# Spilled tiles reloaded four steps ahead, 24 modulation columns moved to the first stage, eight more early tiles in the first placing

## The chip, the cores and the metric

The kernel runs as one program on one core of a Trainium2 chip. The metric is the device time of one execution in microseconds (us); before the change it is 2992.85 us, the median of three runs (2987.78 to 2998.39). All sizes are fixed: 512 tokens and a width of 1024.

## The reference, cut to what matters

Two transformer blocks follow each other. The first mixes tokens by differential attention and a gated linear recurrence, and then runs an expert layer (PEER): every token takes 8 x 16 of 16384 experts, and each expert is one row of `peer_u` and one row of `peer_v`. The second block is modulated by a vector `c`: nine slices of `silu(c) @ w_ada + b_ada` shift, scale and gate its three parts.

```python
def peer_ffn(h, w_query, subkeys, u_table, v_table):      # one block of 128 tokens
        ...                                               # experts and gates by two top-16 searches
        u = u_table[experts]
        hid = jax.nn.gelu(jnp.einsum('nkd,nd->nk', u, xb).astype(jnp.float32), approximate=False) * gates
        return jnp.einsum('nk,nkd->nd', hid.astype(xb.dtype), v_table[experts])
...
    c_act = jax.nn.silu(c)
        mod = c_act @ w_ada[l] + b_ada[l]
        (sh1, sc1, g1, sh2, sc2, g2, sh3, sc3, g3) = jnp.split(mod, N_MOD, axis=-1)
        h = modulate(rmsnorm_2(x, norm_ffn1[l]), sh1, sc1)
```

## The kernel before

Every dense product is made of three TensorE passes: weights and activations are split into a rounded part and its rest (`whi`/`wlo`, `xh`/`xl`, lines 223 to 235). A weight tile is a 128 x 1024 block of 512 KB. SyncE (SP) issues its load into one of three `raw` buffers, ScalarE (ACT) casts it to `whi` (L226), VectorE (DVE) subtracts to get `wlo` (L227), and TensorE (PE) runs its matmuls.

The **first stage** projects the tokens for four heads (`rec_proj`, four weight tiles a head), then runs attention and the recurrence.

The **expert layer** treats 384 of the 512 tokens densely and the other 128 sparsely. The dense way multiplies all 16384 experts: 128 U tiles (`u_chunk`, 24 matmuls, then a GELU on ACT, L725) and 128 V tiles (`down`, 36 matmuls in pairs, L960). Between them the hidden values `ge` are multiplied with a gate matrix on DVE (L945) and split again (`hh` on ACT, L298; `hl` on DVE, L299). The gate matrix is not there from the start: DVE searches the top 16 (`select`), and `place` writes the gates of four tokens at a time into a dense block `stg` (DVE makes two one-hot blocks, ACT scales, PE multiplies, ACT copies out, L885). Every eight such steps the 2 MB of `stg` are stored to `g_d` in HBM (L887). There are three placings of 32 steps.

So that PE has work meanwhile, 80 of the 128 U tiles are made early and their `ge` spilled to `e_d` (192 KB each, `early_u`): 14 during and after the first search, one at every second placing step (48), and the last 18 after the placings. The **main loop** then goes over 128 tiles. At step i it makes or reloads `ge` of tile i (`hidden`), runs `down(i - 3)`, and takes a share of the sparse part. A reload was issued in the step that uses it, into the pool that also holds the fresh GELU outputs:

```python
                if i in done:
                    ge = tp.tile([P, TD], F, name="ge", tag="w")
                    nc.sync.dma_start(ge, e_d[done[i]])
```

Of each eight tiles the five at places 1, 2, 4, 5 and 7 are spilled. The **sparse part** gathers rows of `u` and `v` for the other 128 tokens: 256 gathers of 512 KB (GpSimd, POOL, L747), each followed by one DVE instruction (L756, L764). `sparse` paces them: 32 by the end of the placings, two with each of the 18 late U tiles, the rest spread over the main loop.

The **modulation columns** are 72 products of a 512 KB tile of `w_ada` with the broadcast `silu(c)` (`ada`: a DMA that ACT issues into a `raw` buffer, one DVE instruction, L672). 24 of them stood in the main loop, 48 in the next stage, the first feed-forward layer. `load_c` loads and activates `c`, once behind the placings and once in front of that layer.

Each engine runs its instructions in one fixed order, which a scheduler makes when the program is built; a wait at the head holds back what is behind it. SP's DMA issues also stand in one such order: all weight tiles, the spills and the reloads.

Of the kernel before, what the change touches and what calls it, by code (L numbers as in the profile page):

```python
# [5 lines left out]
P = 128  # L6
T = 512
NM = 16
TE = T + NM
D = 1024  # L10
# [6 lines left out]
EVU = 2  # L17
TD = T - P
# [4 lines left out]
LAG = 2  # L23
LAG2 = 3
LA = 3
NEG = -1.0e30
LAM_INIT = 0.8 - 0.6 * math.exp(-0.3 * 0)
D_FF = 2816
# [131 lines left out]
def program(tc, A, dbg=None, stop=None):  # L160
    import concourse.bass as bass
    from concourse import mybir
    F = mybir.dt.float32
# [4 lines left out]
    AF = mybir.ActivationFunctionType  # L168
    OP = mybir.AluOpType
    AX = mybir.AxisListType  # L170
    PSUM = bass.MemoryType.PSUM
    nc = tc.nc
# [8 lines left out]
    with root:  # L181
# [35 lines left out]
        lastlo = []  # L217
# [37 lines left out]
        class Norm:  # L255


            def __init__(self, nk, pool=nrm, name="nacc", eng=G):
                self.nk, self.eng = nk, eng
                self.acc = pool.tile([P, T], F, name=name, bufs=1)  # L260
                self.k = 0

            def add(self, src, scale=1.0):
# [40 lines left out]
        def stats(pst, sq, tiles, first, last):  # L304
            for j, (c, n) in enumerate(tiles):
                M.matmul(pst[:n, j:j + 1], sq[:, c:c + n], ones[:, 0:1], start=first and j == 0,
                         stop=last, skip_group_check=True)


        with ExitStack() as es:  # L310
# [212 lines left out]
            def rec_proj(h):  # L523
                o = proj(True)
                n1 = first_norm() if h == 0 else iter(())
                next(n1, None)
                o2 = proj(False)
                next(n1, None)
                f = rp.tile([P, TE], F, name="f")
                scaled(f, o)  # L530
                S.activation(f, f, AF.Sigmoid)
                V.tensor_scalar(f, f, oml[:, h:h + 1], lb[:, h:h + 1], op0=OP.mult, op1=OP.add)

                def silu(dst, o):
                    V.tensor_mul(dst, o, rbs[:, :T])
                    sg = tp.tile([P, T], F, name="sg", tag="w", bufs=4)
                    S.activation(sg, dst, AF.Sigmoid)
                    G.tensor_mul(dst, sg, dst)

                q, rg = qr[:, h], qr[:, 4 + h]  # L540
                silu(q, o2)
                vn = to_nat("vr", rp, 4)
                silu(rg, proj(False))
                rec.append((f, q, vn, rg))

            def hgrn(h):
# [69 lines left out]
                split(mh[:, 4 + h], ml[:, 4 + h], y)  # L616
                dump("rec", y, h)

            for h in range(4):
                rec_proj(h)  # L620
                if h == 0:
                    lvm = cp.tile([P, 8, P], U8, name="lvm")
                    for i in range(2):
                        cst = tp.tile([P, T], F, name="lvs", tag="w", bufs=4)
                        nc.scalar.dma_start(cst, A["levels"][:, i * T:(i + 1) * T])
                        V.tensor_copy(lvm[:, i * 4:i * 4 + 4].rearrange("p a b -> p (a b)"), cst)
# [29 lines left out]

        def res(k):
            return xT[:, k]

        cact = []  # L660

        def load_c(pool):
            cb = pool.tile([P, D], F, name="cb", bufs=1)
            nc.scalar.dma_start(cb, A["c"].to_broadcast([P, D]))
            S.activation(cb, cb, AF.Silu)
            cact[:] = [cb]

        def ada(i0, i1):
            for i in range(i0, i1):
                raw = wraw.tile([P, D], F, name="raw")  # L670
                nc.scalar.dma_start(raw, A["w_ada"][i])
                V.scalar_tensor_tensor(raw, raw, 1.0, cact[0], op0=OP.mult, op1=OP.mult,  # L672
                                       accum_out=mod[:, i:i + 1])

        def bias_mod(i0, i1):
            a0, _ = COL_AT["b_ada"]
# [9 lines left out]
        with ExitStack() as es:  # L686
# [35 lines left out]
            def u_chunk(i):  # L722
                o = gemm8(pa, A["peer_u"][i], xh, xl, "a", TD)
                ge = tp.tile([P, TD], F, name="ge", tag="w")
                S.activation(ge, o[:, :TD], AF.Gelu)  # L725
                return ge

            done = {}
# [37 lines left out]
            def sparse(want, step):  # L766

                want = int(min(want, 2 * P))
                while gat[0] < want or (want == 2 * P and gat[1] < want):
                    if gat[0] - gat[1] > lag[0] or gat[0] == 2 * P:  # L770
                        with tc.issue_after(step.ins):
                            use(gat[1])
                        gat[1] += 1
                    if gat[0] < 2 * P:
                        gather(gat[0])
                        gat[0] += 1
# [124 lines left out]
            for t in range(3):  # L901
                for n, _ in enumerate(place(t)):
                    if t < 2:
                        next(nxt, None)
                    if t == 0 and n % 4 == 0:
                        next(nxt, None)
                    if n % EVU == EVU - 1:
                        early_u()
                    sparse(RW[t][0] + RW[t][1] * (n + 1) / 32, placed[0])
            for _ in nxt:  # L910
# [6 lines left out]
            vd = ExitStack()  # L917
            pv = vd.enter_context(tc.tile_pool(name="p1v", bufs=1, space=PSUM))
            rw2 = es.enter_context(tc.tile_pool(name="p1w2", bufs=GB2))
            load_c(hq)  # L920
            nr, nr2 = Norm(8), Norm(8, hq, "nacc2")
            n0 = NU - len(done)
            for _ in range(n0):
                early_u()
                sparse(gat[0] + 2, lastlo[0])
            sp = gat[0]
            pools = [rwp] * GB + [rw2] * GB2
            lag[0] = LAG2
# [5 lines left out]
            def hidden(i):  # L934

                if i % 4 == 0:
                    nc.scalar.dma_start(gts[:, i // 4 % 2].rearrange("p g i n -> p (g i n)"),
                                        g_d[i // 4].rearrange("j g x -> j (g x)"))
                if i in done:
                    ge = tp.tile([P, TD], F, name="ge", tag="w")  # L940
                    nc.sync.dma_start(ge, e_d[done[i]])
                else:
                    ge = u_chunk(i)
                g3 = ge.rearrange("p (g n) -> p g n", n=TG)
                gated[:] = [V.tensor_mul(g3, g3, gts[:, i // 4 % 2, :, i % 4])]  # L945
                hh_ = hq.tile([P, TD], R, name="hh", bufs=LA + 2)
                hl_ = hq.tile([P, TD], R, name="hl", bufs=LA + 2)
                split_alt(i, hh_, hl_, ge)
                hid[i] = hh_, hl_

            def down(i):

# [2 lines left out]
                for t in range(3):  # L955
                    sl = slice(t * P, (t + 1) * P)
                    for x_, w, st, en in ((hh_, hi, i == 0, False), (hl_, hi, False, False),
                                          (hh_, lo, False, i == P - 1)):
                        for j in range(2):
                            M.matmul(acc[t * 2 + j], x_[:, sl], w[:, j * T:(j + 1) * T], start=st, stop=en,  # L960
                                     skip_group_check=True)

            for i in range(P + LA):
                if i < P:
                    hidden(i)
                if i >= LA:
                    down(i - LA)
                if i < P:
                    ada(24 * i // P, 24 * (i + 1) // P)
                    sparse(sp + (2 * P - sp) * cost[i] / cost[P - 3], gated[0])  # L970
            ys = [rwp.tile([P, D], F, name="rows") for t in range(3)]
            for t in range(3):
                for j in range(2):
                    (V.tensor_copy if j else S.copy)(ys[t][:, j * T:(j + 1) * T], acc[t * 2 + j])
            ys += ya
            vd.close()
            ps = es.enter_context(tc.tile_pool(name="p1e", bufs=2, space=PSUM))
            for m in range(8):
# [498 lines left out]
```

## Time and profile before

| what | before |
|---|---|
| median of three runs | 2992.85 us |
| the profiled execution | 2989.74 us |
| its span, first to last instruction | 2987.9 us |
| mean granted clock of PE in it | 0.972 |
| PE busy | 2813.1 us (94%) |
| DVE busy | 1910.7 us (64%) |
| ACT busy | 1160.2 us (39%) |
| POOL busy | 478.4 us (16%) |
| moved by DMA | 522.25 MB, 175 GB/s on average |

The profile is one execution. A busy share is an average over stages that have different limits. The granted clock is the share of the full rate that the throttle gave PE: 1.00 is 2.4 GHz, half of it 1.2 GHz. An idle time stands in brackets with what ended it: `[4.31 <-DVE wlo L227]` says that the engine had waited 4.31 us for that result.

### The profile page before, as it was taken

The page shows a single profiled execution, that of the slowest core. Times are in us where ns is not written, and L with a number is a line of the kernel's source. Part 1 is how long each engine was busy: PE and PEld are TensorE (multiplying, and loading weights), DVE is VectorE, ACT ScalarE, POOL GpSimd, SP SyncE. Part 2 cuts the span into 40 slices and gives each one's busy share as a digit, 9 for nine tenths or more (in the row PEclk, how much of TensorE's full clock was granted, in tenths as well). Part 3 has the DMA queues.
Part 4 walks back from the last instruction along what each step waited for, and adds up shares of the span by engine and source line. Part 5 has one row for each costly group of instructions (what it writes and reads, how often), then busy time and mean ns, then how long its engine had stood idle before and what let it go on. Part 6 is the DMA issues. An engine that isn't in the chain of part 4 may idle for free. (4 is left out here: it accounts for less than half of the span.)

```text
span 2987.9 us, 37696 instructions
## 1 busy us (share of the span) xinstructions
PE 2813.1 (94%) x14087; PEld 2394.2 (80%) x14087; DVE 1910.7 (64%) x3461; ACT 1160.2 (39%) x2003; POOL 478.4 (16%) x353
## 2 busy tenths in 40 slices
PE   8999999988996899998998997999999999999998
PEld 7878779878996788877877876888878777788876
DVE  5577489999775688766777674554457645533332
ACT  3233333566772233333333334222245626422222
POOL 2000100000133333333334322000110000200000
PEclk9999999999998999999999998999999999999999
DMA  4201223456899899988988862555522102233332
GB/s 146 78 29 36 79 85 113 136 165 197 275 318 345 308 356 340 323 307 290 320 290 312 311 224 85 171 174 173 167 91 74 50 30 64 78 99 93 97 92 73
DMA packets 201303, 522.25 MB, mean 175 GB/s; under 512 B 17184, under 2 KB 88992, under 8 KB 200992
## 3 DMA queue, kind: packets, MB, share of 16 engines
q1 hardware_dynamic: 96480, 290.56, 29.7%
q0 software_dynamic: 36864, 134.23, 12.6%
q10 hardware_dynamic: 67776, 95.04, 9.4%
q8 instruction: 111, 1.82, 0.3%
q14 instruction: 72, 0.59, 0.1%
HBM read 476.78 MB, written 42.99 MB: 174 GB/s over the span
## 5 line engine op out<-in xcount | busy, mean ns | idle before, releaser
L226 ACT CAST whi<-raw 128x1024 fp32r<-128x1024 f32 (+2 forms) x500 | 512.2, 1029 | 904.2 <-PE o L234 579.5
L233 PE MATMUL o<-xh,whi 128*128 128x512 f32 (+1 forms) x2064 | 762.7, 371 | 31.0 <-ACT ge L725 26.7
L235 PE MATMUL o<-xh,wlo 128*128 128x512 f32 (+1 forms) x2064 | 760.5, 369 | 24.7 <-DVE wlo L227 24.5
L227 DVE TENSOR_TENSOR wlo<-raw,whi 128x1024 fp32r<-128x1024 f32 (+2 forms) x500 | 592.4, 1197 | 276.8 <-ACT whi L226 267.6
L234 PE MATMUL o<-xl,whi 128*128 128x512 f32 (+1 forms) x2064 | 759.3, 368 | 1.3 <-DVE xl L1018 0.7
L233 PEld LDWEIGHTS o<-xh,whi 128*128 128x128 f32 x2064 | 395.0, 192 | 79.8 <-ACT ge L725 30.1
L235 PEld LDWEIGHTS o<-xh,wlo 128*128 128x128 f32 x2064 | 394.4, 191 | 71.8 <-DVE wlo L227 30.6
L234 PEld LDWEIGHTS o<-xl,whi 128*128 128x128 f32 x2064 | 394.4, 191 | 47.0 <-DVE xl L1018 2.5
L960 PE MATMUL acc<-wlo,hh 128*128 128x512 f32 x768 | 243.7, 399 | 33.7 <-DVE wlo L227 33.7
L747 POOL DMA_INDIRECT rows<-u_rows,eg x128 | 160.5, 1254 | 690.6 <-DVE rows L756 459.2
L747 POOL DMA_INDIRECT rows<-v_rows,eg x128 | 189.4, 1480 | 346.3 <-DVE ya L764 327.8
L960 PE MATMUL acc<-whi,hl 128*128 128x512 f32 x768 | 241.5, 396 | 2.3 <-DVE hl L299 2.3
L960 PE MATMUL acc<-whi,hh 128*128 128x512 f32 x768 | 242.0, 397 | 1.5 <-ACT hh L298 1.5
L271 POOL TENSOR_TENSOR nacc<-nacc,nsq 128x512 f32<-128x512 f32 x47 | 68.0, 1456 | 1028.8 <-ACT nsq L268 586.2
L298 ACT CAST hh<-ge 128x384 fp32r<-128x384 f32 x128 | 65.8, 514 | 396.3 <-DVE ge L945 388.4
L960 PEld LDWEIGHTS acc<-wlo,hh 128*128 128x128 f32 x768 | 146.5, 192 | 69.7 <-DVE wlo L227 39.4
L672 DVE SCALAR_TENSOR_TENSOR raw<-raw,cb 128x1024 f32<-128x1024 f32 x72 | 89.2, 1238 | 149.6 <-DMA raw<-w_ada 149.6
L756 DVE SCALAR_TENSOR_TENSOR rows<-rows,xn 128x1024 f32<-128x1024 f32 x128 | 155.5, 1221 | 38.2 <-DMA rows<-u_rows,eg 38.0
L960 PEld LDWEIGHTS acc<-whi,hl 128*128 128x128 f32 x768 | 147.3, 192 | 34.3 <-DVE hl L299 2.6
L960 PEld LDWEIGHTS acc<-whi,hh 128*128 128x128 f32 x768 | 147.1, 192 | 29.7 <-ACT hh L298 1.8
L945 DVE TENSOR_TENSOR ge<-ge,gts 128x384 f32<-128x384 f32 x128 | 71.0, 554 | 156.1 <-DMA ge<-e_d 156.1
L764 DVE SCALAR_TENSOR_TENSOR ya<-rows,hg,ya 128x1024 f32<-128x1024 f32 x127 | 162.4, 1279 | 0.0
(455 smaller groups left out, 4076.1 us busy)
## 6 DMA issues: line engine op xcount, KB each, us to landing
raw<-peer_u SPq DMA_DIRECT2D x128, 512.0 KB
raw<-v_rows SPq DMA_DIRECT2D x128, 512.0 KB
raw<-w_ada ACTq DMA_DIRECT2D x72, 512.0 KB
raw<-w_in SPq DMA_DIRECT2D x54, 512.0 KB
g_d<-stg ACTq DMA_DIRECT2D x12, 2048.0 KB
gts<-g_d ACTq DMA_DIRECT2D x32, 768.0 KB
e_d<-ge SPq DMA_DIRECT2D x80, 192.0 KB
ge<-e_d SPq DMA_DIRECT2D x80, 192.0 KB
```

Of the source, the lines that this page charges most:

```text
L226: S.copy(hi[:, :n], raw[:, :n])
L227: lastlo[:] = [V.tensor_sub(lo[:, :n], raw[:, :n], hi[:, :n].bitcast(F))]
L233: M.matmul(out, a, xh, start=first, stop=False, skip_group_check=True)
L234: M.matmul(out, a, xl, start=False, stop=False, skip_group_check=True)
L235: M.matmul(out, b, xh, start=False, stop=last, skip_group_check=True)
L271: self.eng.tensor_add(self.acc, self.acc, sq)
L672: V.scalar_tensor_tensor(raw, raw, 1.0, cact[0], op0=OP.mult, op1=OP.mult, accum_out=mod[:, i:i + 1])
L747: G.indirect_dma_start(out=rw, out_offset=None, in_=A["u_rows" if s < P else "v_rows"], in_offset=bass.IndirectOffsetOnAxis(ap=eg[:, s % P ...
L756: V.scalar_tensor_tensor(rw, rw, 1.0, xn, op0=OP.mult, op1=OP.mult, accum_out=h)
L764: V.scalar_tensor_tensor(ya[0], rw, h, ya[0], op0=OP.mult, op1=OP.add)
L945: gated[:] = [V.tensor_mul(g3, g3, gts[:, i // 4 % 2, :, i % 4])]
L960: M.matmul(acc[t * 2 + j], x_[:, sl], w[:, j * T:(j + 1) * T], start=st, stop=en, skip_group_check=True)
```

## The change

A reload is now issued four steps ahead of its use (`LE = 4`, `reload`) into a pool of its own with four buffers, `ges`. `load_c` is called in the first stage: it puts `silu(c)` into two rows of `qr` that the fourth head fills later. The first 24 modulation columns follow the projections of heads 0, 1 and 2, eight each, and SP issues their loads. The main loop has no `ada` and the placings' end no `load_c` any more. In the first placing a U tile is also made at every fourth step, so that placing has 24 instead of 16, and 10 instead of 18 are left for the time after the placings. There one gather instead of two goes with each of them, so the main loop starts with 42 gathers done instead of 68. The accumulator of the second norm takes a `rows` buffer. The numbers of what is computed do not change.

```diff
+LE = 4
...
+        def load_c(pool, cb=None):
+            if cb is None:
+                cb = pool.tile([P, D], F, name="cb", bufs=1)
+            src = A["c"].to_broadcast([P, D])
+            nc.scalar.dma_start(cb, src if len(cb.shape) == 2 else src.rearrange("p (a t) -> p a t", a=2))
+            S.activation(cb, cb, AF.Silu)
+            cact[:] = [cb]
+
+        def ada(i0, i1, eng=nc.scalar):
+            for i in range(i0, i1):
+                raw = wraw.tile([P, D], F, name="raw")
+                eng.dma_start(raw, A["w_ada"][i])
+                rv = raw if len(cact[0].shape) == 2 else raw.rearrange("p (a t) -> p a t", a=2)
+                V.scalar_tensor_tensor(rv, rv, 1.0, cact[0], op0=OP.mult, op1=OP.mult,
+                                       accum_out=mod[:, i:i + 1])
...
+            load_c(None, qr[:, 3::4])
             for h in range(4):
                 rec_proj(h)
+                if h < 3:
+                    ada(8 * h, 8 * h + 8, nc.sync)
...
-                    if n % EVU == EVU - 1:
+                    if n % EVU == EVU - 1 or t == 0 and n % 4 == 0:
                         early_u()
...
-            load_c(hq)
-            nr, nr2 = Norm(8), Norm(8, hq, "nacc2")
             n0 = NU - len(done)
             for _ in range(n0):
                 early_u()
-                sparse(gat[0] + 2, lastlo[0])
+                sparse(gat[0] + 1, lastlo[0])
...
-                if i in done:
-                    ge = tp.tile([P, TD], F, name="ge", tag="w")
-                    nc.sync.dma_start(ge, e_d[done[i]])
-                else:
-                    ge = u_chunk(i)
+                ge = spilled.pop(i) if i in done else u_chunk(i)
...
+            spilled = {}
+
+            def reload(i):
+                if i in done:
+                    spilled[i] = hq.tile([P, TD], F, name="ges", bufs=4)
+                    nc.sync.dma_start(spilled[i], e_d[done[i]])
...
+            for i in range(LE):
+                reload(i)
             for i in range(P + LA):
+                reload(i + LE)
                 if i < P:
                     hidden(i)
                 if i >= LA:
                     down(i - LA)
                 if i < P:
-                    ada(24 * i // P, 24 * (i + 1) // P)
                     sparse(sp + (2 * P - sp) * cost[i] / cost[P - 3], gated[0])
...
+            nr, nr2 = Norm(8), Norm(8, acc=rw2.tile([P, D], F, name="rows")[:, :T])
```

Three places of the engines' orders show what moves. The first is the start of SP's order, where all loads of the first stage stand; before:

```order
L195 DMA raw<-w_in 128x1024
L199 DMA x0T<-xT 128x528 x8
L223 DMA raw<-w_in 128x1024 x27
L223 DMA raw<-w_out 128x1024 x8
L223 DMA raw<-w_query 128x1024 x16
```

And after:

```order
L196 DMA raw<-w_in 128x1024
L200 DMA x0T<-xT 128x528 x8
L224 DMA raw<-w_in 128x1024 x3
L323 DMA raw<-w_ada 128x1024 x8
L224 DMA raw<-w_in 128x1024 x4
L323 DMA raw<-w_ada 128x1024 x8
L224 DMA raw<-w_in 128x1024 x4
L323 DMA raw<-w_ada 128x1024 x8
L224 DMA raw<-w_in 128x1024 x16
L224 DMA raw<-w_out 128x1024 x8
```

Eight loads of modulation columns now stand in front of the four weight tiles of heads 1, 2 and 3, in the same three `raw` buffers.

The second place is ACT's order at the end of the last placing, from the last copy into `stg` on (`gts` is the gate block that is read back from `g_d`); before:

```order
L885 COPY stg<-pg 128x128x4 x2
L887 DMA g_d<-stg 128x32x128
L725 ACTIVATE ge<-o 128x384
L226 CAST whi<-raw 128x1024 x2
L664 DMA cb<-c 128x1024
L725 ACTIVATE ge<-o 128x384
L937 DMA gts<-g_d 128x1536
L665 ACT_TABLE_LOAD
L665 ACTIVATE cb<-cb 128x1024
L725 ACT_TABLE_LOAD
L725 ACTIVATE ge<-o 128x384 x2
```

And after:

```order
L892 COPY stg<-pg 128x128x4 x2
L894 DMA g_d<-stg 128x32x128
L732 ACTIVATE ge<-o 128x384
L227 CAST whi<-raw 128x1024 x2
L732 ACTIVATE ge<-o 128x384
L942 DMA gts<-g_d 128x1536 x2
L732 ACTIVATE ge<-o 128x384
L227 CAST whi<-raw 128x1024 x2
```

The load of `c`, its activation and two table loads are gone; the read of `gts` comes one GELU later than the load of `c` stood, and nothing but that GELU stands between.

The third place is DVE's order in the middle of the main loop (`hl` is the rest of a gated tile, `ya` the sparse sum; `ge` is a fresh or a reloaded tile before, a fresh one after, where reloaded ones are named `ges`); before:

```order
L945 TENSOR_TENSOR ge<-ge,gts 128x384
L764 SCALAR_TENSOR_TENSOR ya<-rows,hg,ya 128x1024
L299 TENSOR_TENSOR hl<-ge,hh 128x384 x2
L764 SCALAR_TENSOR_TENSOR ya<-rows,hg,ya 128x1024
L945 TENSOR_TENSOR ge<-ge,gts 128x384
L764 SCALAR_TENSOR_TENSOR ya<-rows,hg,ya 128x1024
L227 TENSOR_TENSOR wlo<-raw,whi 128x1024
L299 TENSOR_TENSOR hl<-ge,hh 128x384
L227 TENSOR_TENSOR wlo<-raw,whi 128x1024
L672 SCALAR_TENSOR_TENSOR raw,mod<-raw,cb 128x1024
L227 TENSOR_TENSOR wlo<-raw,whi 128x1024 x2
```

And after:

```order
L300 TENSOR_TENSOR hl<-ges,hh 128x384
L771 SCALAR_TENSOR_TENSOR ya<-rows,hg,ya 128x1024
L300 TENSOR_TENSOR hl<-ges,hh 128x384
L771 SCALAR_TENSOR_TENSOR ya<-rows,hg,ya 128x1024
L228 TENSOR_TENSOR wlo<-raw,whi 128x1024
L771 SCALAR_TENSOR_TENSOR ya<-rows,hg,ya 128x1024
L228 TENSOR_TENSOR wlo<-raw,whi 128x1024
L946 TENSOR_TENSOR ges<-ges,gts 128x384
L228 TENSOR_TENSOR wlo<-raw,whi 128x1024 x2
L946 TENSOR_TENSOR ge<-ge,gts 128x384
L771 SCALAR_TENSOR_TENSOR ya<-rows,hg,ya 128x1024
L300 TENSOR_TENSOR hl<-ge,hh 128x384
```

The L672 row is gone, and the gate multiply of a reloaded tile stands between the `wlo` of weight tiles. Every `hl<-ges` frees one of the four buffers for the reload that is fourth behind it; here the gate multiply next behind the second `hl<-ges` comes two `ya` and two `wlo` later.

## Rows read from the trace of the kernel before

**Rows 1.** Busy time by stretch: start:end, length, then engines, clock, DMA share, GB/s.

```profile
core 0: us, PE busy (x) PEld busy (x) DVE busy (x) ACT busy (x) POOL busy (x), PEclk, DMA share, GB/s
0.00:140.00 140.00, 128.16 (x806) 114.74 (x807) 77.17 (x134) 46.21 (x66) 24.05 (x19) 1.00 0.37 119
551.00:677.00 126.00, 108.01 (x618) 100.56 (x618) 124.89 (x310) 80.98 (x190) 3.46 (x3) 0.93 0.47 148
888.00:1019.00 131.00, 95.99 (x491) 92.15 (x490) 71.10 (x98) 36.27 (x49) 49.48 (x37) 0.90 0.91 324
1019.00:1788.00 769.00, 732.70 (x3407) 632.88 (x3407) 572.29 (x732) 256.37 (x350) 260.97 (x186) 0.98 0.86 310
1100.00:1200.00 100.00, 100.00 (x479) 87.31 (x478) 81.59 (x124) 37.20 (x49) 39.51 (x29) 1.00 0.92 337
```

**Rows 2.** What PE waited for from 888 to 1019 us: total, times, longest.

```profile
PE o L233 <- ACT ge L725: 21.3, 4, 15.0
PE o L235 <- DVE wlo L227: 12.6, 7, 4.8
```

**Rows 3.** ACT's timeline there: start, duration, instruction, idle before and its releaser.

```profile
888.68 0.38 ACTq L887 DMA_DIRECT2D g_d<-stg  x1
...
912.05 0.35 ACTq L664 DMA_DIRECT2D cb<-c  x1
912.45 0.49 ACT L725 ACTIVATE ge<-o 128x384 f32<-128x384 f32 x1 [17.66 <-DMA g_d<-stg]
```

**Rows 4.** SP's timeline there: two rows that follow each other.

```profile
890.26 0.33 SPq L736 DMA_DIRECT2D e_d<-ge  x1
912.03 0.33 SPq L223 DMA_DIRECT2D raw<-v_rows  x1
```

**Rows 5.** The GELUs from 912 to 1019 us: ns min/median/max, first and last start.

```profile
L725 ACT ACTIVATE ge<-o x19: 478/484/492, 912.4 to 1015.7; 128x384 f32<-128x384 f32 x19
```

**Rows 6.** What DVE and PE waited for in the main loop, 1019 to 1788 us.

```profile
DVE ge L945 <- DMA ge<-e_d: 156.1, 42, 7.7
DVE wlo L227 <- ACT whi L226: 34.0, 19, 3.2
...
PE acc L960 <- DVE wlo L227: 33.7, 13, 6.1
```

**Rows 7.** One stall of the main loop in the timeline: SP, PE and DVE.

```profile
1401.50 1.37 SPq L941 DMA_DIRECT2D ge<-e_d  x2
...
1410.33 0.33 PE L233 MATMUL o<-xh,whi 128*128 128x384 f32 x1
...
1413.14 0.56 DVE L945 TENSOR_TENSOR ge<-ge,gts 128x384 f32<-128x384 f32 x1 [7.58 <-DMA ge<-e_d]
...
1414.49 0.62 PE L960 MATMUL acc<-whi,hh 128*128 128x512 f32 x2
...
1419.88 1.22 PE L960 MATMUL acc<-wlo,hh 128*128 128x512 f32 x2 [4.31 <-DVE wlo L227]
...
1420.90 1.05 PE L960 MATMUL acc<-whi,hh 128*128 128x512 f32 x2
```

**Rows 8.** DVE's groups on the page: count, busy us, mean ns, idle before.

```profile
L227 DVE TENSOR_TENSOR wlo<-raw,whi 128x1024 fp32r<-128x1024 f32 (+2 forms) x500 | 592.4, 1197 | 276.8 <-ACT whi L226 267.6
...
L672 DVE SCALAR_TENSOR_TENSOR raw<-raw,cb 128x1024 f32<-128x1024 f32 x72 | 89.2, 1238 | 149.6 <-DMA raw<-w_ada 149.6
L756 DVE SCALAR_TENSOR_TENSOR rows<-rows,xn 128x1024 f32<-128x1024 f32 x128 | 155.5, 1221 | 38.2 <-DMA rows<-u_rows,eg 38.0
```

**Rows 9.** The first stage's timeline: two tiles one head apart, and one load.

```profile
36.73 1.05 ACT L226 CAST whi<-raw 128x1024 fp32r<-128x1024 f32 x1 [4.42 <-PE pj L400]
...
43.84 0.33 ACTq L625 DMA_DIRECT2D lvs<-levels  x1
...
46.39 0.43 DVE L626 CAST lvm<-lvs 128x512 uint8<-128x512 f32 x1 [1.16 <-DMA lvs<-levels]
...
60.19 1.05 ACT L226 CAST whi<-raw 128x1024 fp32r<-128x1024 f32 x1 [4.23 <-PE pj L400]
```

More of the change, by code (lines that the diff above doesn't have):

```diff
@@ L255, in program, with __init__ @@
         class Norm:
-            def __init__(self, nk, pool=nrm, name="nacc", eng=G):
+            def __init__(self, nk, pool=nrm, name="nacc", eng=G, acc=None):
                 self.nk, self.eng = nk, eng
-                self.acc = pool.tile([P, T], F, name=name, bufs=1)
+                self.acc = pool.tile([P, T], F, name=name, bufs=1) if acc is None else acc
                 self.k = 0
@@ L307, in stats @@
                          stop=last, skip_group_check=True)
+        cact = []
+        def load_c(pool, cb=None):
[12 more added lines that the diff above has]
+                                       accum_out=mod[:, i:i + 1])
         with ExitStack() as es:
@@ L658, in res @@
             return xT[:, k]
[L660 to L673, printed above, removed]
         def bias_mod(i0, i1):
```

## The prediction

> **What bounds the kernel now.** I read the busy time by stretch first, then in each stretch that the change touches what ended the waits, and the timeline only where a wait needed a cause. In all of them the reader should look for the engine without idle time, since only its work is on the path.
>
> The first stage is PE's: 128.16 of 140.00 us at clock 1.00, while DVE works 77.17 [rows 1]. The first placing (551 to 677) is DVE's: 124.89 of 126.00, PE 108.01 at 0.93 [rows 1]. Behind the placings (888 to 1019) no engine is full: PE 95.99 of 131.00 at 0.90, but DMA 0.91 and 324 GB/s [rows 1]. That stretch starts with a hole: ACT issues a store of `g_d` at 888.68, has the load of `c` next, which waits for the stores until 912.05, and the GELU behind it starts after 17.66 us of idle time [rows 3]; PE waits up to 15.0 us for that `ge` [rows 2]. SP, too, issues nothing from 890.26 to 912.03 [rows 4]. Then 19 GELUs follow in 103.3 us, 18 intervals of 5.74 us [rows 5].
>
> The main loop (1019 to 1788) has PE busy 732.70 of 769.00 at 0.98 [rows 1]; at full clock and without idle time that work is 732.7 x 0.98 = 718 us, so 51 us are to be had. DVE's 572.29 busy [rows 1], 156.1 waiting for reloads in 42 waits and 34.0 for `whi` [rows 6] make 762 of 769: DVE never has time in hand, because a reload at its head stops it. One stall shows how that reaches PE [rows 7]: reloads issued at 1401.50, DVE released at 1413.14 (11.6 us later), `wlo` late, PE idle 4.31 us and then a pair of matmuls in 1.05 instead of 0.62 us. Where DVE keeps up (1100 to 1200) PE is busy 100.00 of 100.00 at 337 GB/s [rows 1].
>
> **The change part by part.**
>
> *Modulation columns in the first stage.* 24 loads and 24 DVE instructions of 1.238 us [rows 8] = 29.7 us; DVE has 140.00 - 77.17 = 62.8 us free [rows 1], so nothing need show. No wait goes and nothing is taken out here, so it can't be below 0. But eight loads go ahead of each head's four weight tiles through the same three buffers, in a head of 60.19 - 36.73 = 23.46 us; a load of half the size lands 46.39 - 43.84 = 2.55 us after its issue [rows 9]. With the products one after another, 24 x (2.55 + 1.24) = 91 us less the free 63, it is +28. It is nearer to nothing, as DVE's free time is twice its new work; I take one landing seen in each of three heads, 3 x 2.55 = **+8**.
>
> *Eight more U tiles in the first placing.* DVE, the bound, gets eight `wlo`, 8 x 1.197 = 9.6 us [rows 8]. PE gets 8 x 4.16 (one U tile, 1410.33 to 1414.49 [rows 7]) = 33.3 us and has 18.0 idle [rows 1], so with all of these filled it needs 15.3 more. Ends: 9.6 and, with no idle time usable, 33.3. PE and DVE would be about equally full, and a fuller PE may get back part of the 0.93; I take **+14**.
>
> *Behind the placings.* Eight tiles of 5.74 us leave: -45.9. Gathers fall from two with each of 18 tiles to one with each of 10, 26 fewer. The stretch moves 131 us x 324 GB/s = 42.4 MB [rows 1]; 26 gathers of 0.52 MB, eight weight tiles of 0.52 and their spills of 0.2 take 19.4 MB out, at the same rate -60 us. If DMA is no limit any more, 103.3 becomes 10 x 4.16 = 41.6, -62, and the load of `c`, its activation and the table loads leave too: PE's waits for `ge` are 21.3, 15.0 of them the hole [rows 2], so -6.3 at most. The hole stays: the read of `gts` waits for the same stores, one GELU later in ACT's order. Ends: -33 (PE's 8 x 4.16 alone) and -68; I take **-62**, as bytes and PE's floor agree within 8 us.
>
> *Main loop, DVE's work.* Out go 24 products, 24 x 1.238 = 29.7 us; in come the uses of 26 gathers, 26 x 1.221 = 31.7 us [rows 8]. The bytes go the same way, 12.6 MB out and 13.6 in. Nothing either way, and PE covers it: DVE without the reload waits would need 606 of 718 us.
>
> *Main loop, reloads.* Four steps are 24 us (769/128 = 6.0 each), twice the 11.6 us landing. But the pool has four buffers, so a reload can't be issued before the `hl` of the fourth reload before it. I counted DVE's order between that `hl` and the gate multiply which needs the tile: for three of five tiles in each period of eight, two to four instructions, 3 to 5 us; for the other two about 14 us. So two of five land in time, 0.4 x 51 = 20 us, and the other three keep some 8 of their 11.6 us wait, 0.6 x 51 x 0.3 = 9. Ends: 0 and -51; I take **-30**. New on SP: the reload now waits for an `hl` at the head of the queue, with the loads of V and U tiles behind it, and PE waits for these.
>
> Of how long a transfer takes, row and rule differ. The trace shows 11.6 us for a reload of 192 KB under load [rows 7]. The Trainium skill, "DMA: Bandwidth & Descriptors", section "Anatomy of one DMA — SWDGE (gpsimd) path", fits 2.0 us plus bytes / 436e3 for a single DMA issued from GpSimd (these come from SP): an estimate of 2.45 us, by which even the short leads suffice and the loop goes to its floor. By the trace they don't.
>
> The rest (accumulators created later, one in a `rows` buffer) issues nothing in a full stretch.
>
> Sum: 8 + 14 - 62 - 30 = -70. The profiled execution took 2989.74 us, 3.1 below the median of 2992.85, so 2989.74 - 70 + 3.1 = **2923**.
>
> **The rivals.**
>
> *The ring is too short everywhere.* DVE's waits for reloads keep their size since `hl` frees a buffer too late; loop 0. For it: the 3 to 5 us leads. Against: the other two of five. 2923 + 30 = 2953.
>
> *Every reload lands in time.* The 11.6 us of [rows 7] is a peak in a crowded moment, and the usual landing is like the 2.55 us of [rows 9]. Loop -51: 2923 - 21 = 2902. Against: the longest of 42 waits is 7.7, their mean 156.1/42 = 3.7 [rows 6], so ordinary ones are late too. The rule of the Trainium skill weighed above would give this result.
>
> *The first stage is held by its buffers:* +28 instead of +8, 2943.
>
> *The moved U tiles bring nothing:* the placing grows by 33 and the tail loses 33. For it: at 0.93 PE is not idle because of lack of work alone. 2923 + 48 = 2971.
>
> *No effect:* the loop's wait moves from DVE to SP's queue, the tail's bytes only move into the loop. About 2993.
>
> *Slower, by SP's queue.* A reload that waits for `hl` holds the V tile's load behind it. From that `hl` PE has three V tiles of (718 - 48 x 4.16)/128 = 4.05 us and a U tile of 4.16 before the V tile is needed, 16.3 us; landing 11.6, cast 1.05 [rows 9] and `wlo` 1.2 take 13.9. If landing takes over 14 us, PE stalls in each of 16 periods, as in [rows 7]: 4.3 idle and six pairs at 1.05 instead of 0.62, about 7 us; 16 x 7 = +112 in place of -30: 3065. For it: SP did stand 21.8 us behind one waiting instruction [rows 4]. The Trainium skill, same page and section, says that DMA engines don't wait on semaphores, the issuing sequencer does before dispatch; the gap of [rows 4] agrees. Against: buffers come free in the order of use, and DVE gets there sooner when it waits less.
>
> **How the numbers follow.** The forecast has 0.46, the short ring 0.18, all in time 0.13, slower by SP 0.07, the first stage 0.06, no gain from the moved tiles 0.05, no effect 0.05. The forecast's own range is 2900 to 2945 (tail and placing by some 10 each way, the loop from -15 to -45). The range for all, 2882 to 2960, reaches on one side to the loop at -51 with the tail at -68 and the placing at +9.6 and the stage at 0 (2881), on the other past the short ring; outside lie no gain from the moved tiles, no effect and SP, 0.17, and little else. What a measurement of this kernel can tell from no change is about 0.3%, 9 us. Faster: 0.46 + 0.18 + 0.13 + 0.06 + 0.05 = 0.88; same 0.05; slower 0.07.
>
> **What would show it.** First stage: head period near 26 us, with PE waiting for `wlo` or `whi` behind late `raw` loads. Placing: near 140 us, DVE and PE both full, a higher clock. Tail: some 69 us, the hole of 15 us still there behind the last `g_d` store. Loop: DVE's wait for `e_d` well under 156 us but not gone, and sitting at three of five tiles; PE idle near 15. Wrong would be: waits of `wlo` behind V loads that SP issued late (the slower rival), reload waits of the old size, or a tail that keeps over 100 us.

## The result, and the profile after

The changed kernel takes 2952.51 us, the median of four runs (2945.64 to 2953.95), beside 2995.07 us for the kernel before, here the median of four runs: a ratio of 0.9857 with a 95% interval of 0.9832 to 0.9881. That is 42.6 us faster, where 70 were forecast. The profiled execution has a span of 2950.8 us, 37.1 below that of before.

The starts of named instructions cut both profiled executions into stages: the first matmul into `pg` (the first placing begins), the fourth and the twelfth store of `g_d`, the first matmul of `down` and its last one with `hl`.

| stage, us | before | after | difference | forecast |
|---|---|---|---|---|
| up to the first placing | 550.0 | 564.0 | +14.0 | +8 |
| first placing | 126.6 | 138.9 | +12.3 | +14 |
| second and third placing | 212.1 | 211.9 | -0.2 | 0 |
| behind the placings | 130.7 | 78.1 | -52.6 | -62 |
| main loop | 768.0 | 757.0 | -11.0 | -30 |
| the rest | 1200.5 | 1200.9 | +0.4 | 0 |

Busy time by stretch, with the columns of [rows 1]; the last two rows are the main loop in two parts:

```profile
core 0: us, PE busy (x) PEld busy (x) DVE busy (x) ACT busy (x) POOL busy (x), PEclk, DMA share, GB/s
0.00:154.00 154.00, 133.34 (x810) 117.90 (x811) 106.68 (x186) 49.49 (x71) 24.97 (x19) 0.97 0.59 194
564.00:703.00 139.00, 131.83 (x816) 128.76 (x814) 137.68 (x332) 92.13 (x206) 3.73 (x3) 0.98 0.55 175
915.00:993.00 78.00, 55.17 (x298) 53.28 (x296) 35.64 (x47) 20.70 (x29) 16.95 (x14) 0.90 0.83 307
993.00:1750.00 757.00, 728.52 (x3406) 629.23 (x3407) 572.01 (x724) 251.96 (x349) 300.99 (x208) 0.98 0.86 314
993.00:1310.00 317.00, 290.12 (x1317) 246.75 (x1318) 216.90 (x327) 95.56 (x136) 108.95 (x81) 0.96 0.81 291
1310.00:1750.00 440.00, 438.40 (x2091) 382.47 (x2090) 355.11 (x397) 156.40 (x213) 192.03 (x127) 1.00 0.90 331
```

The placing came out as expected, with DVE and PE both nearly full and the clock up from 0.93 to 0.98. The loop is now two loops. From 1310 us on PE is idle for 1.6 us in all. Nearly all that is lost is lost before that, where PE idles 27 of 317 us at a lower clock while DVE is busy for only 217. What DVE and PE waited for in that first part:

```profile
DVE rows L763 <- DMA rows<-u_rows,eg: 56.9, 22, 5.6
DVE ges L946 <- DMA ges<-e_d: 20.6, 9, 4.5
DVE ges L946 <- DMA gts<-g_d: 16.7, 7, 4.3
...
PE acc L968 <- DVE wlo L228: 23.2, 11, 5.7
PE acc L968 <- ACT hh L299: 12.5, 1, 12.5
```

Over the whole loop the waits for reloads fell from 156.1 us [rows 6] to 33.0:

```profile
DVE ges L946 <- DMA ges<-e_d: 33.0, 18, 4.5
```

In their place stand waits for gathered rows of `u`, of which the loop of the kernel before shows none. The timeline shows what is odd about them (POOL issues gathers, DVE uses them):

```profile
1069.19 1.68 POOL L754 DMA_INDIRECT rows<-u_rows,eg  x1 [6.47 <-DVE rows L763]
...
1075.84 1.01 POOL L754 DMA_INDIRECT rows<-u_rows,eg  x1 [0.60 <-DVE rows L763]
...
1084.87 1.23 DVE L763 SCALAR_TENSOR_TENSOR rows<-rows,xn 128x1024 f32<-128x1024 f32 x1 [1.57 <-DMA rows<-u_rows,eg]
...
1087.16 1.22 DVE L763 SCALAR_TENSOR_TENSOR rows<-rows,xn 128x1024 f32<-128x1024 f32 x1
```

The use at 1084.87 waits for the semaphore of the gather of 1075.84, while the gather issued at 1069.19 is used only at 1087.16, without a wait. The order of DVE shows why (buffer numbers rise in the order in which the program was written; `...` stands for rows left out):

```
L946 TENSOR_TENSOR ges_9967<-ges_9967,gts_9262 128x384
L946 TENSOR_TENSOR ges_10038<-ges_10038,gts_9262 128x384
L763 SCALAR_TENSOR_TENSOR rows_9962,hg_3345<-rows_9962,xn_3346 128x1024
...
L763 SCALAR_TENSOR_TENSOR rows_10105,hg_3345<-rows_10105,xn_3346 128x1024
L763 SCALAR_TENSOR_TENSOR rows_10172,hg_3345<-rows_10172,xn_3346 128x1024
...
L946 TENSOR_TENSOR ge_10001<-ge_10001,gts_9262 128x384
L763 SCALAR_TENSOR_TENSOR rows_9927,hg_3345<-rows_9927,xn_3346 128x1024
...
L763 SCALAR_TENSOR_TENSOR rows_9930,hg_3345<-rows_9930,xn_3346 128x1024
```

`sparse` queues each use behind the gate multiply of its step. With the reload ahead, the multiply of a reloaded tile (`ges_10038`) is scheduled before that of the fresh tile of an earlier step (`ge_10001`), and the uses go with it: `rows_9962` to `rows_10172` are waited for before `rows_9927`, whose gather came first. Of the 60 uses of `u` rows from the 69th on, 54 stand at another place than their gather. Before the change there are 2, the uses of the 35th and the 38th gather, which come late. Uses of `v` rows add up into `ya` one after the other and can't change places, and the second part of the loop is clean: the last use of a `u` row starts at 1320.4 us.

### The profile page after: what moved, and what is told of

It reads as the page before. It is cut to its first block, busy times and chain, and to the rows that moved or that the text cites. A ratio compares the mean times of both kernels' runs of the same rounds, so it can differ in the third digit from the quotient of the medians.

```text
span 2950.8 us, 37658 instructions
## 1 busy us (share of the span) xinstructions
PE 2799.6 (95%) x14087; PEld 2383.8 (81%) x14087; DVE 1912.9 (65%) x3461; ACT 1154.4 (39%) x2002; POOL 485.3 (16%) x353
## 3 DMA queue, kind: packets, MB, share of 16 engines
q0 software_dynamic: 36864, 134.23, 12.5%
## 5 line engine op out<-in xcount | busy, mean ns | idle before, releaser
L968 PE MATMUL acc<-whi,hh 128*128 128x512 f32 x768 | 241.0, 395 | 16.1 <-ACT hh L299 12.5
L272 POOL TENSOR_TENSOR nacc<-nacc,nsq 128x512 f32<-128x512 f32 x41 | 59.3, 1446 | 1030.7 <-ACT nsq L269 590.5
L968 PEld LDWEIGHTS acc<-wlo,hh 128*128 128x128 f32 x768 | 145.6, 191 | 60.8 <-DVE wlo L228 30.7
L325 DVE SCALAR_TENSOR_TENSOR raw<-raw,cb 128x1024 f32<-128x1024 f32 x48 | 60.4, 1258 | 140.3 <-DMA raw<-w_ada 140.3
L234 PE MATMUL o<-fh,whi 128*128 128x512 f32 x352 | 139.5, 396 | 0.0
L236 PE MATMUL o<-fh,wlo 128*128 128x512 f32 x352 | 138.7, 394 | 0.0
## 6 DMA issues: line engine op xcount, KB each, us to landing
gts<-g_d ACTq DMA_DIRECT2D x32, 768.0 KB
```

Source lines behind the costliest of these rows:

```text
L234: M.matmul(out, a, xh, start=first, stop=False, skip_group_check=True)
L236: M.matmul(out, b, xh, start=False, stop=last, skip_group_check=True)
L272: self.eng.tensor_add(self.acc, self.acc, sq)
L325: V.scalar_tensor_tensor(rv, rv, 1.0, cact[0], op0=OP.mult, op1=OP.mult, accum_out=mod[:, i:i + 1])
```

## The experiments

Stages are cut as above, each from one profiled execution. Loop and tail (behind the placings) in us. Each ratio is to the kernel before, measured in the same set of runs:

| kernel | median | ratio to before, 95% | tail | loop |
|---|---|---|---|---|
| changed, uses in order | 2891.72 | 0.9662 (0.9622 to 0.9702) | 65.2 | 713.6 |
| columns moved only | 2943.76 | 0.9841 (0.9800 to 0.9882) | 122.3 | 715.9 |
| changed, reload in its step | 2907.28 | 0.9708 (0.9669 to 0.9747) | 67.8 | 727.7 |
| changed, no early tiles more | 2985.62 | 0.9972 (0.9949 to 0.9994) | 137.0 | 746.6 |
| columns moved, products put back | 2943.53 | 0.9822 (0.9784 to 0.9859) | 127.3 | 715.7 |
| columns moved, loads put back | 3008.31 | 1.0051 (1.0028 to 1.0074) | 129.8 | 776.9 |
| the same, loads by SP | 2964.19 | 0.9887 (0.9842 to 0.9931) | 125.7 | 729.7 |
| the same, loads in an own buffer | 2987.53 | 0.9970 (0.9951 to 0.9989) | 135.1 | 745.7 |
| before, reloads by ACT | 2937.71 | 0.9794 (0.9750 to 0.9838) | 129.7 | 713.0 |
| before, reloads by ACT, early tiles | 2884.58 | 0.9643 (0.9620 to 0.9666) | 66.0 | 714.3 |

**Uses in order.**

Each use of a `u` row is queued behind the use before it (`used` holds that instruction):

```diff
...
+                            if used:
+                                ia.enter_context(tc.issue_after(used[0].ins))
                             use(gat[1])
...
```

> The changed kernel, with each use of a gathered u row queued behind the use before it. Theory A (the reload ahead let the scheduler put the uses of the newest gathers ahead of older ones, so DVE waits for gathers that have just been issued, 56.9 us in the first third of the loop): those waits fall below 10 us, the first third of the loop goes from 317 to about 285 us, the kernel from 2952.5 to 2915 to 2930. Theory B (the loop simply has too many gathers for its first third, in any order): waits change name, the time stays within 5 of 2952. Theory C (the ring of four buffers holds the loop): the waits for reloads and gate blocks, 33 and 23 us, stay and grow, gain below 10 us.

It took 2891.72 us, 61 less than the changed kernel: theory A, with 23 us more gain than the best that it said. The loop runs at PE's floor, the time of a PE that is never idle at clock 1.00, and the waits for `u` rows are gone (the loop's row, then DVE's waits):

```profile
972.00:1686.00 714.00, 714.00 (x3408) 623.49 (x3406) 574.94 (x730) 256.48 (x347) 307.76 (x212) 1.00 0.92 335
...
DVE ges L951 <- DMA ges<-e_d: 30.1, 21, 4.3
...
DVE rows L765 <- DMA rows<-u_rows,eg: 2.6, 2, 1.4
```

The tail is 13 us shorter too. Theory C falls: the 30 us of waits for reloads are still there and cost PE nothing.

**Columns moved only** (reload and early tiles as before).

> The kernel before with only the modulation columns moved (24 products and c's load in the first stage; no early tiles more, reloads in their step). First stage +14 as in the changed kernel; tail -6 (no load of c); loop: DVE loses 30 us of work but still stops at each reload. Theory A and C: loop -5 to -10, so 2993 to 2999. Rival (DVE's work in the loop was the limit): loop -25 or more, so below 2980.

The rival's time came true: 2943.76, and the loop of 768.0 fell to 715.9 with the reloads still in their step and none of them ahead.

```profile
1019.00:1735.00 716.00, 715.64 (x3406) 624.57 (x3407) 549.05 (x684) 264.21 (x349) 233.11 (x186) 1.00 0.89 316
...
DVE ge L950 <- DMA ge<-e_d: 28.5, 27, 3.8
```

PE is never idle, and the waits for reloads have gone from 156.1 to 28.5 us. So the reload's step alone is not their cause. Whether it was DVE's work, as the rival says, or the loads, is tested below.

**Reload in its step, and no early tiles.** The first gives back the lines of before in `hidden` and drops the calls of `reload`; the second:

```diff
-                    if n % EVU == EVU - 1 or t == 0 and n % 4 == 0:
+                    if n % EVU == EVU - 1:
...
-                sparse(gat[0] + 1, lastlo[0])
+                sparse(gat[0] + 2, lastlo[0])
```

> The changed kernel with the reloads back in their step (columns moved, eight more early tiles). The uses stand in order here. Theory A: front part as in the changed kernel (stage +14, placing +12, tail -52), loop some 5 us longer than before for 26 gathers more less 24 columns: 2965 to 2980, and DVE's waits are for reloads (about 150 us), none for u rows. If the gathers themselves are too many (B), DVE waits for u rows here too and the loop is 790 us or more: 2990.

> The changed kernel without the eight early tiles (18 tiles behind the placings, two gathers with each, 68 gathers done when the loop starts). The uses are out of order here as well, but only 60 u rows are left for the loop. Theory A: DVE waits some 40 us for u rows in the loop, loop about 750: 2975 to 2985. Theory B: with 26 gathers fewer in the loop the waits for u rows go away, and the loop reaches 725 to 735: about 2960.

The first missed by over 55 us on the good side (2907.28), because theory A took the columns for nearly worthless in the loop; its waits for `u` rows are 0.6 us, as theory A says. The second (2985.62, loop 746.6) is as A expected, with its waits for `u` rows in the loop:

```profile
DVE rows L763 <- DMA rows<-u_rows,eg: 55.4, 20, 6.0
```

The four kernels give the parts of the change: columns -48 us (2943.76 beside 2991.31 for the kernel before in the same set of runs), early tiles with their gathers -36 (2943.76 to 2907.28), reload ahead +42 to +45 (2943.76 to 2985.62, and 2907.28 to 2952.51). The part meant for the loop is the one that loses; with the uses in order the same part gains 16 (2907.28 to 2891.72).

**What in the 24 columns cost the loop 52 us.** Products without loads, then loads without products:

```diff
+                    for _ in range(24 * i // P, 24 * (i + 1) // P):
+                        V.scalar_tensor_tensor(xn, xn, 1.0, xn, op0=OP.mult, op1=OP.max)
```

```diff
+                        raw = wraw.tile([P, D], F, name="raw")
+                        nc.scalar.dma_start(raw, A["w_ada"][j])
+                        V.tensor_copy(junk, raw[:, 0:1])
...
```

> The kernel with only the columns moved (2943.8 us, main loop 715.9 with PE never idle), and 24 products of the same size put back into the loop at the places of the removed ones, on data that is in SBUF (they leave their operand as it is): DVE's work is back, the 24 loads are not. Theory D (DVE had no slack: 30 us of work in an order that waits at every reload is what cost the loop 52 us): loop 745 to 768, the kernel 2973 to 2996. Theory R (the loads were the cost: each takes one of three weight buffers): loop 716 to 725, the kernel below 2953.

> The kernel with only the columns moved, and the 24 loads of 512 KB put back into the loop (into the same three weight buffers, issued by ACT), each freed by a copy of one column instead of the product; the columns themselves are made in the first stage. Theory R: loop 745 to 768, the kernel 2973 to 2996. Theory D: loop 716 to 725, below 2953.

By the times it is theory R: 2943.53 with the products, 3008.31 with the loads. DVE's 30 us of work cost nothing; each load costs 61.0/24 = 2.5 us (loop 776.9 against 715.9). The waits for reloads come and go with the loads, here in the loop of the kernel with loads:

```profile
DVE ge L951 <- DMA ge<-e_d: 178.5, 42, 10.6
...
PE acc L973 <- DVE wlo L228: 44.2, 14, 7.9
...
SPq L224 <- DVE wlo L228: 615.5, 124, 19.2
```

SP stands 615.5 of 777 us before a weight load whose buffer isn't free, and reloads stand behind these. The kernel before has the same wait, and its stall of [rows 7] shows the order: SP issued nothing from 1384.8 to 1397.27, then four weight loads, and then the reloads of 1401.50.

```profile
SPq L223 <- DVE wlo L227: 602.4, 132, 16.5
...
1383.66 1.12 SPq L941 DMA_DIRECT2D ge<-e_d  x2
1397.27 1.94 SPq L223 DMA_DIRECT2D raw<-v_rows  x2
```

**The loads by SP; the loads in a buffer of their own; the reloads by ACT.** One word or line each (`nc.sync` for `nc.scalar`; `hq.tile(..., name="araw", bufs=1)` for the tile of `wraw`); the third is the kernel before with

```diff
-                    nc.sync.dma_start(ge, e_d[done[i]])
+                    nc.scalar.dma_start(ge, e_d[done[i]])
```

> The kernel with the 24 loads and no products in the loop (loop 776.9 us, 3008 us), the loads issued by SP instead of ACT; the columns are made in the first stage. If the cost is the weight buffer that each load holds (one of three, for landing and until its turn on DVE): loop still 760 to 780, 2990 to 3010. If it was ACT's queue, where an issue waits for a buffer in front of the casts: loop 716 to 730, below 2960. If it is the 12.6 MB, no change either, told apart by the next run.

> The same 24 loads in the loop, issued by ACT, into a buffer of their own of 512 KB; the columns are made in the first stage. If the cost is the weight buffer: loop 716 to 725, 2940 to 2955. If it is the bytes (12.6 MB at 316 GB/s are 40 us of transfer) or ACT's queue: loop 755 to 780, above 2985.

> The kernel before with one word changed: ACT issues the reloads, in their step, instead of SP. If reloads were late because they stood on SP behind weight loads that wait for a buffer: DVE's waits for them fall from 156 to below 60 us, loop 720 to 745, the kernel 2945 to 2975. If they were late because of the transfer, or because the weight loads themselves are what is late: waits and loop within 10 of before, 2985 to 3000. Against the first: ACT too runs in order, and a reload that waits for its buffer there holds the casts.

The third is beyond its best case in time, though DVE's waits for reloads stayed just above the 60 us expected: 2937.71, the loop at 713.0, with the columns still in it.

```profile
1020.00:1733.00 713.00, 713.00 (x3403) 622.76 (x3402) 571.17 (x729) 260.09 (x348) 270.13 (x185) 1.00 0.91 333
...
DVE ge L945 <- DMA ge<-e_d: 63.3, 33, 4.1
...
SPq L223 <- DVE wlo L227: 603.2, 147, 16.0
```

SP waits as long as ever, but no reload is behind it. This shows that the time was lost where two things meet: reloads on SP behind weight loads that wait for a buffer, and 24 more loads in the ring of three buffers. Take either away (713.0 here, 715.9 with the columns moved) and the loop is at PE's floor. The loads cost nothing by themselves: here they stand in the loop, in the same buffers and issued by ACT. What it does not show is that the late issue was all of DVE's wait. In the traces, the 42 reloads that DVE waited for in the kernel before were issued on average 4.2 us before DVE was ready for them and released it 7.9 us after their issue. With the columns moved these are 27 reloads with 6.7 and 7.8 us: the issue came earlier. With the reloads on ACT they are 33 with 5.0 and 6.9 us: the flight got shorter by about as much as the issue got earlier. Whether another queue or less traffic in front made it shorter was not tested.

The first two fit no theory whole. Issued by SP, the loads cost 14 us instead of 61 though they hold the same buffers (the loop of 729.7 is what was expected for ACT's queue, the time of 2964.19 is 4 us above it). In a buffer of their own they still cost 30, with a new wait of DVE and one of ACT, which stands before the issue of a load until that one buffer is free:

```profile
DVE junk L985 <- DMA araw<-w_ada: 44.8, 7, 7.9
DVE ge L951 <- DMA ge<-e_d: 36.3, 24, 6.9
...
ACT whi L227 <- DVE junk L985: 21.0, 7, 3.3
```

Few reloads are late there, but the one buffer's load is. How much of the 61 us comes by the buffer held and how much by the place in ACT's order, as long as SP issues the reloads, stays open.

**The hole behind the placings, and the bunch of eight in the first stage** (both on the changed kernel with uses in order). The first holds back the reads of `gts`, the first reloads and, not shown here, the first V tiles; the second puts two columns behind each projection:

```diff
...
+                        if i < 8:
+                            ia.enter_context(tc.issue_after(hold[0]))
...
+            with tc.issue_after(hold[1]):
+                for i in range(LE):
+                    reload(i)
```

```diff
...
             silu(q, o2)
+            two()
             vn = to_nat("vr", rp, 4)
+            two()
...
```

> The changed kernel with the uses in order (2891.7 us) and, behind the placings, the first two reads of gts, the first four reloads and the first three V tiles queued behind the fifth of the ten late U tiles, so that neither ACT nor SP stands before the g_d stores while U tiles can be made. If the hole costs the path what PE waits there: it goes, the stretch from the last g_d store to the first down tile goes from 65 to 50 to 55 us, the kernel to 2877 to 2882. Rival: the wait only moves behind the fifth tile, since the stores take 18 us to land and the ten tiles 42: within 4 us of 2892.

> The changed kernel with the uses in order, and the 24 columns two behind each of the twelve projections of heads 0 to 2 instead of eight behind each head. If the bunch of eight is what holds vt on DVE (PE waited 8.2 us for it, three times 4.0 at most): the first stage loses 5 to 10 us, the kernel 2882 to 2887. Rival: the three buffers are the limit, and any place among the projections costs the same 9 to 14 us: 2889 to 2895.

Both rivals: 2888.74 and 2892.74, not to be told from 2891.72. In the first PE's wait for `ge` fell from 9.7 to 6.6 us and the tail from 65.2 to 60.8; in the second the wait for `vt` from 7.6 to 4.4, and 5.8 us of waiting for `kk` came instead.

**A smaller change.** The kernel before with the reloads issued by ACT, the eight early tiles and one gather for two in the tail; no columns moved, no reload ahead.

> The kernel before with three lines changed: ACT issues the reloads in their step, eight more U tiles in the first placing, one gather instead of two with each of the ten tiles behind the placings; the columns stay in the loop. If the columns need not move once the reloads are off SP: first stage as before (550 us), placing +10, tail about 73, loop 714 to 720, so 2880 to 2895. Rival: with 26 gathers more, the columns and the reloads of ACT, the loop leaves PE's floor (742 us or more): above 2910.

2884.58 us (2882.33 to 2892.11), as expected where the columns need not move, and the shortest of all, though its interval and that of the kernel with uses in order overlap. The first stage is as before (552.2 us up to the first placing) and the loop as full as it gets:

```profile
966.00:1681.00 715.00, 714.02 (x3408) 623.46 (x3406) 602.28 (x784) 259.53 (x349) 306.08 (x212) 1.00 0.94 352
```

## Why the prediction was right, and where its steps failed

**Right in direction and within the range, for partly wrong reasons.** Its number matches the rival of the short ring (2953), and that is chance: that rival wanted the waits for reloads to keep their size, and they fell to a fifth. It was luck, too, that the total lies in the range. The loop gave -11.0 in place of -30, in parts that were not forecast: -52.1 for the columns, +11.8 for the early tiles with their gathers, +29.3 for the reload ahead (768.0, 715.9, 727.7, 757.0). One small sum is also off: the lower end adds up to 2883 and not to 2881.

**"Main loop, DVE's work: nothing either way."** This step failed most. I weighed the products against the gathers' uses and counted the loads only as bytes. The products were indeed worth nothing, but taking out the 24 loads was worth 52 us while SP issued the reloads, in one order with weight loads that wait for the same three buffers. With the reloads on ACT the same loads cost nothing. SP's 602.4 us of waiting for weight buffers was in the profile before; I read DVE's wait for the reload and not what the reload's issue had stood behind.

**"Main loop, reloads: -30."** As built the step lost 29 to 31 us of loop (715.9 to 746.6, 727.7 to 757.0) and 10 to 15 us of tail. The ring of four, on which I spent the working, didn't matter: 30.1 us of such waits stand beside a PE that is never idle. What I missed is in the changed order itself, in the buffer numbers: a wait that goes away lets a multiply move up, and what is queued behind that multiply moves with it. The stall at 1401 us [rows 7] was read rightly as 11.6 us from issue to landing, but it was no usual landing, and SP's 12.5 us without an issue in front of it were not read. In the changed kernel the 18 reloads that DVE waited for released it 6.3 us after their issue on average.

**"Every reload lands in time"** was given 0.13. The waits for reloads after the change, 33.0 us in 18 cases, are nearer to none than to mine of 8 us in three of five tiles, so most leads did suffice. The estimate of 2.45 us for the landing, from the Trainium skill, "DMA: Bandwidth & Descriptors", section "Anatomy of one DMA — SWDGE (gpsimd) path", is not borne out for these DMAs. In the changed kernel it was the 6.3 us above for those that were waited for, and 6.7 us (median) where ACT issued the reloads. On the loop's time this rival was as wrong as the forecast: the floor was reached only with the uses in order.

**First stage +8: mis-sized.** It measured +14.0, and +9 to +16 in the nine other kernels with the same first stage. PE waited 8.2 us for `vt`, which before cost it 0.2, and where these waits lie the clock was lower (0.90 from 50 to 100 us, PE busy 43.5 of 50; 1.00 and 50.0 before). The rows of after and before:

```profile
PE pn L438 <- DVE vt L430: 8.2, 3, 4.0
...
PE pn L419 <- DVE vt L411: 0.2, 1, 0.2
```

I had priced late landings; the trace puts the waits on DVE, whose order has products ahead of `vt`. That this order is the cost isn't shown: with the columns spread, PE waited for `kk` instead and the time stayed.

**First placing +14, tail -62:** +12.3 as forecast. The tail gave -52.6 as built, but -65.5 with the uses in order and -62.9 with the reload in its step, so the sum was right and ten to thirteen of it went to misplaced uses. DVE stood 6.2, 7.2 and 5.5 us for three gathers at the end of the tail, and PE 12.5 us for the `hh` behind them:

```profile
DVE rows L763 <- DMA rows<-u_rows,eg: 18.9, 3, 7.2
```

The hole stayed (a GELU waited 12.5 us for the stores of `g_d`, beside 17.66 [rows 3]), and queuing the reads and loads later to shorten it was worth nothing that can be measured.

**"Slower, by SP's queue"** looked at the right queue from one side only: weight loads held back reloads on SP in the kernel before. After the change SP does stand before reloads, 186.6 us for `hl`, but with the uses in order it is 204.5 us beside a PE that is never idle.

## What to carry to other kernels

A wait for a transfer has two halves, the issue and the flight. Before an issue is moved ahead, look what stands in front of it in its queue: another queue may do the same with one word. And when a change takes a wait away from an instruction, look for everything that is ordered behind that instruction, and whether it is still in the order in which its inputs arrive.

## What the runs showed that was not expected

An in-order issuer that waits 600 of 770 us hides the fact in the waits of others: the same 80 reloads cost DVE 156.1 us of waiting issued by SP and 63.3 us issued by ACT, and PE 55 us of loop (768.0 to 713.0). The Trainium skill, "DMA: Bandwidth & Descriptors", section "Issuing engines are not separate DMA queues", says that issuing on several engines only saves the sequencers' time to issue, usually small beside the transfer. The rate did not change by much (310 and 333 GB/s), which agrees; the gain was not small here: 55 us of loop. An issue that waits for a buffer holds the ones behind it on that engine. The same page's section "Anatomy of one DMA — SWDGE (gpsimd) path" puts the semaphore wait on the issuing sequencer, before dispatch, and SP's 602.4 us of waits agree.

24 loads of 512 KB cost 61 us issued by ACT, 14 by SP and 30 into one buffer of their own; the products that they feed, 24 x 1.24 us on the engine that was taken for the loop's limit, cost nothing. With the reloads on ACT the loads cost nothing either.
